# Host-laid inputs for the beginning, shift and scale in four parts, late roots in both norms

## The chip, the cores and the metric

The kernel runs on one core of one Trainium2 chip. The metric is the device time in microseconds (us) of one execution, as the median over runs; what is done to the inputs on the host before the launch is not in it. The engines of the core work side by side, each in its own queue's order: TensorE (matmul, transposes), VectorE, ScalarE, GpSimd (POOL) and SyncE (SP), which issues most of the loads.

## The reference, cut to what matters

One layer of a trunk over 512 latent tokens `x` and 256 context tokens `ctx`, 1024 channels. The condition vectors `c` and `c_ctx` give six modulation rows each (shift, scale, gate, twice). The parts that the change touches:

```python
mod  = split(silu(c) @ w_mod + b_mod, 6);  modc = split(silu(c_ctx) @ w_mod + b_mod, 6)
h    = modulate(rmsnorm(x, norm1_g), mod[0], mod[1])        # h * (1 + scale) + shift
hc   = modulate(rmsnorm(ctx, norm1_g), modc[0], modc[1])
u    = split(h @ w_in, ...)    ; uc = split(hc @ w_in, ...)   # mLSTM, attention, SSD, gates
y_m, y_a, y_s = mlstm(u, uc), diff_attention(u, uc), ssd(u, uc)
x    = x + mod[2] * (gated sum of y_m @ w_m, y_a @ w_a, y_s @ w_s) @ w_out
h2   = modulate(rmsnorm(x, norm2_g), mod[3], mod[4])
x    = x + mod[5] * conv_ffn(h2 @ w_up) @ w_down
rmsnorm(x, g) = x * rsqrt(mean(x * x) + 1e-6) * g
```

## The kernel before, in words

All large products keep f32 accuracy by splitting both factors into a high part in the short f32 format (fp32r) and a low rest, and adding three matmuls (high·high, high·rest, rest·high). A weight piece (`wpiece`, `wcol`, `wblk`) is loaded by SP into `wr` (two buffers), its high part `wh` is made by ScalarE (L171) and its rest `wl` by VectorE (L85); `wh` and `wl` have four buffers each. A helper records each operation, so nearly all matmuls have line L82, activations L104, two-input products L85, products with a scalar and a second input L88.

The beginning, lines 216 to 388, has these steps. The tokens come in rows (`xs`, three loads of 1 MB). Their squares are summed on ScalarE, the root is taken on VectorE (`rstd`, twelve small operations), the rows are scaled, and 48 transposes on TensorE turn them into columns (`xT`, channels on the partitions). Shift and scale need `silu(c) @ w_mod`: eight pieces of 0.5 MB (`wm`, five buffers) for each of two stages (NS = 2), multiplied with 32 columns of `scl` in 64 matmuls a stage, four of them side by side in strips of 32 rows. `h_part(n)` turns the sums into columns (`MT`, `A1`), and gives for each block of 128 channels k the high part of h (ScalarE) and the rest (VectorE), for the latent tokens (512 columns, `hlat`) and the context (256, `hctx`). Small parameters come by some twenty small loads (`crow`, `prm`, `wgr`) in rows, and are turned by three transposes (`PT`); the gate columns of `w_in` are copied one by one into a padded tile `wg`.

Four projections, called early, are begun while shift and scale are still being made: the gates (latent and context), a key column block (latent and context) and two query blocks (latent). Their matmuls for the k of stage n run beside the sums of stage n + 1 (`early(n)`). After them the mLSTM branch goes on with dense projections. The gate rows (`gate_rows`) run on VectorE and ScalarE beside these.

The second norm, lines 1118 to 1190: the output projection goes over blocks of 256 columns and token tiles j; each result is added to x1 on VectorE, and its squares are summed on ScalarE. `norm2(half)` takes the root for two token tiles, scales x1 into `xn`, transposes it (16 transposes a half) and makes high part and rest of h2 from the transposed tile. Half 0 is placed before the last block of the output projection, half 1 before the second half of the first four up projections, whose four banks (`fps`) are held until their convolutions have been read by VectorE. A tile `fc` for the last modulation row takes the buffer of `xn` (tag hc); its 16 products with w_mod run on VectorE beside the first up projections.

A list scheduler with a model of the engines places each operation in its engine's queue in the order in which it would be ready, with a higher priority for what stands in `tc.high_priority(...)`, and not before another one where `tc.issue_after(...)` says so. On the chip each queue is then worked off in that fixed order.

Of the kernel before, what the change touches and what calls it, by code (L numbers as in the profile page):

```python
# [18 lines left out]
P = 128  # L19
D = 1024  # L20
NK = D // P
T = 512
# [16 lines left out]
def build(tc, a, out):  # L39
# [150 lines left out]

    def proj_part(w, pl, pc, ks):
        hi, lo = w
        for k in ks:
            for n, (wt, v) in enumerate(((hi, 0), (hi, 1), (lo, 0))):
                st, sp_ = k == 0 and n == 0, k == NK - 1 and n == 2
                if pl is not None:
                    mm(pl, wt[:, k, :], hlat[v][:, k, :], st, sp_)
                if pc is not None:
                    mm(pc[:, 0:TC], wt[:, k, :], hctx[v][:, k, :], st, sp_)
# [12 lines left out]
    NS, NE, EX = 2, 3, 3  # L212
    W = D // NS
    KW, QW = W // P, W // 256

# [6 lines left out]

    last = [None, None]
# [3 lines left out]
    with pool("ph0", 1) as p0:  # L227

        crow = p0.tile([32, P], F32, name="crow")
        nc.sync.dma_start(crow[0:8, :], a["c"][0].rearrange("(r c) -> r c", c=P))  # L230
        nc.sync.dma_start(crow[8:16, :], a["c_ctx"].rearrange("(r c) -> r c", c=P))
        wv = w_in.rearrange("(k p) c -> p k c", p=P)
        wgr = wgp.tile([P, NK, 32], F32, name="wgr")
        nc.sync.dma_start(wgr[:, :, 0:16], wv[:, :, C_GM:C_GM + 16])
        nc.sync.dma_start(wgr[:, :, 16:32], wv[:, :, C_DT:C_DT + 16])
        xs = p0.tile([P, 6, D], F32, name="xs")
        for i in range(3):
            src = a["ctx"][0] if i == 0 else a["x"][0, (i - 1) * 256:i * 256]
            nc.sync.dma_start(xs[:, 2 * i:2 * i + 2, :], src.rearrange("(j p) c -> p j c", p=P))
            if i == 0:  # L240
                nc.sync.dma_start(crow[16:24, :], a["norm1_g"][0].rearrange("(r c) -> r c", c=P))
                nc.sync.dma_start(crow[24:32, :], a["norm2_g"][0].rearrange("(r c) -> r c", c=P))

        V.memset(scl, 0.0)
        tp = pss()
        PE.transpose(out=tp[:, 0:32], in_=crow, identity=ident[0:32, 0:32])
        act(scl[:, :, 0:2], tp[:, 0:16].rearrange("p (r k) -> p k r", r=2), AF.Silu)
        V.tensor_copy(NG, tp[:, 16:32])

        ssq = p0.tile([P, 6], F32, name="ssq")  # L250
        rs = p0.tile([P, 6], F32, name="rs")
        xT = p0.tile([P, NK, NT], F32, name="xT")
        for i in range(3):
            for t in (2 * i, 2 * i + 1):
                junk = p0.tile([P, D], mybir.dt.bfloat16, tag="junk", name="junk", bufs=1)
                act(junk, xs[:, t, :], AF.Square, accum=ssq[:, t:t + 1])
            rstd(rs[:, 2 * i:2 * i + 2], ssq[:, 2 * i:2 * i + 2], 2, 1.0 / D)
            for t in (2 * i, 2 * i + 1):
                ts(V, xs[:, t, :], xs[:, t, :], rs[:, t:t + 1])
            for k in range(0, NK, 2):  # L260
                tp = pss()
                for n in range(4):
                    PE.transpose(out=tp[:, n * P:(n + 1) * P], in_=xs[:, 2 * i + n % 2, (k + n // 2) * P:(k + n // 2 + 1) * P],  # L263
                                 identity=ident)
                o = xT[:, k:k + 2, i * 256:(i + 1) * 256]
                if k % 4:
                    V.tensor_copy(o, tp.rearrange("p (k c) -> p k c", k=2))
                else:
                    S.copy(o, tp.rearrange("p (k c) -> p k c", k=2))
# [4 lines left out]
        V.memset(wg, 0.0)  # L274
        prm = p0.tile([P, 3, P], F32, name="prm")
        V.memset(prm[:, 2, :], 0.0)
        V.memset(prm[96:128, 0, :], 0.0)

        def prow(which, r0, src):
            G.dma_start(prm[r0:r0 + src.shape[0], which, :], src)  # L280

        def rows(name):
            x = a[name][0]
            if len(x.shape) == 1:
                return x.rearrange("(r c) -> r c", c=P)
            return x.rearrange("k (r c) -> (k r) c", c=P)

        def grow(r, off, src):
            G.dma_start(prm[r:r + 1, 2, :].rearrange("o (d x) -> o d x", x=32)[:, off // 32:off // 32 + 2,
                                                                               off % 32:off % 32 + src.shape[2]], src)  # L290

        prow(0, R_BM, rows("b_mod"))
        prow(0, R_MCW, rows("m_conv_w"))
        prow(0, R_MCB, rows("m_conv_b"))
        prow(0, R_SCW, rows("s_conv_w"))
        prow(0, R_SCB, rows("s_conv_b"))

        prow(2, R3_G + 2, a["rowc"])
        grow(R3_G, 0, a["m_igate_b"])
        grow(R3_G, 64, a["m_fgate_b"])  # L300
        grow(R3_G, 72, a["s_dt_bias"])
        grow(R3_G + 1, 72, a["s_a_log"])
        fr = rows("ffn_conv_w")
        prow(2, 0, fr[128:132])
        prow(2, R3_MN, rows("m_norm_g"))
        prow(2, R3_SN, rows("s_norm_g"))
        prow(2, R3_SUB, a["a_subln_g"])
        prow(1, 0, fr[0:128])

        def pt(w):  # L310
            tp = pss()
            PE.transpose(out=tp[:, 0:P], in_=prm[:, w, :], identity=ident)
            V.tensor_copy(PT[:, w, :], tp[:, 0:P])

        for d in range(2):
            V.tensor_copy(wg[:, :, 32 * d:32 * d + 4], wgr[:, :, d * 8:d * 8 + 4])
            V.tensor_copy(wg[:, :, 64 + 32 * d:68 + 32 * d], wgr[:, :, d * 8 + 4:d * 8 + 8])
            V.tensor_copy(wg[:, :, 72 + 32 * d:80 + 32 * d], wgr[:, :, 16 + d * 8:24 + d * 8])
        split(wgh, wgl, wg)
        def h_part(n):  # L320

            ps = pss() if n else psl()
            for k in range(NK):
                r = p0.tile([P, 2, W], F32, tag="wm", name="wm", bufs=20 // QW // 2)
                last[0] = nc.sync.dma_start(r, a["w_mod"][0, k * P:(k + 1) * P, 0:2 * D]
                                            .rearrange("p (s c) -> p s c", s=2)[:, :, n * W:(n + 1) * W])
                for q in range(2 * QW):
                    last[1] = mm(ps[32 * q:32 * q + 32, 0:256], scl[:, k, :],
                                 r[:, q // QW, (q % QW) * 256:(q % QW + 1) * 256], k == 0, k == NK - 1)
                yield  # L330
            if n == 0:
                pt(0)
            R = 64 * QW
            m = p0.tile([P, 256], F32, tag="xw", name="msb", bufs=3)
            S.copy(m[0:R], ps[0:R, 0:256])
            tp = pss()
            for c in range(2):
                PE.transpose(out=tp[:, c * P:c * P + R], in_=m[0:R, c * P:(c + 1) * P], identity=ident[0:R, 0:R])
            ks = slice(n * KW, (n + 1) * KW)
            for s in (1, 0):  # L340
                for c in range(2):
                    tt(V, MT[:, s, ks].rearrange("p (q c) r -> p q c r", c=2)[:, :, c, :],
                       tp[:, c * P:c * P + R].rearrange("p (q r) -> p q r", r=32)[:, s * QW:(s + 1) * QW, 0:2],
                       PT[:, 0, s * 8 + n * KW:s * 8 + (n + 1) * KW].rearrange("p (q c) -> p q c", c=2)[:, :, c:c + 1]
                       .broadcast_to([P, QW, 2]), ALU.add)
            stt(A1[:, ks], MT[:, 1, ks], 1.0, NG[:, ks].unsqueeze(2).broadcast_to([P, KW, 2]), ALU.add, ALU.mult)
            for k in range(n * KW, (n + 1) * KW):
                for r, cs, h_ in ((0, slice(TC, NT), hlat), (1, slice(0, TC), hctx)):
                    hins[0] = act(h_[0][:, k, :], xT[:, k, cs], AF.Identity, scale=A1[:, k, r:r + 1], bias=MT[:, 0, k, r:r + 1])
                    ts(V, xT[:, k, cs], xT[:, k, cs], A1[:, k, r:r + 1], MT[:, 0, k, r:r + 1], ALU.mult, ALU.add)  # L350
                    tt(V, h_[1][:, k, :], xT[:, k, cs], h_[0][:, k, :].bitcast(F32), ALU.subtract)
            yield

        def early(n):

            for i, e in enumerate(first):
                if n == 0 and i:
                    for e_ in first[i + 1:i + 2]:
                        with tc.issue_after(last[0].ins):
                            e_[0] = wcol(e_[3])  # L360
# [921 lines left out]
```

## Time and profile before

| | |
|---|---|
| median of 3 runs | 1111.38 us (1109.24 to 1113.02) |
| profiled execution | 1112.19 us, span of its instructions 1110.4 us |
| TensorE / its weight loads | 1071.9 us (97%) / 939.2 us (85%) |
| VectorE / ScalarE / GpSimd | 714.6 us (64%) / 474.8 us (43%) / 78.7 us (7%) |
| mean granted TensorE clock | 0.993 |
| moved by DMA | 119.66 MB, 108 GB/s over the span |

An engine's share of busy time is a mean over stages that have different limits. The span is also shown in forty slices of 27.8 us; of these only the first shows TensorE far below nine tenths, four tenths. A row of the list in order of time has the start, the busy time, the engine, the line, the operation with what it writes and reads, the count, and in brackets how long the engine stood idle before it and what ended that.

### The profile page before, as it was taken

Reading aid. Unit: us, or ns where it says so; the run is one execution under the profiler, and the core shown is the slowest. Engines: PE = TensorE matmul, PEld = TensorE weight load, DVE = VectorE, ACT = ScalarE, POOL = GpSimd, SP = SyncE. Lnnn points to the kernel's source line nnn. Section 1 sums busy time; section 2 is a strip of 40 time slices with the busy share of each in tenths; the row PEclk is TensorE's granted clock in tenths of the full one; section 3 lists DMA queues with packets and bytes.
Section 4 is the critical chain, followed back from the end, with each engine's and each line's share of the span. In section 5 each row is a group of like instructions: output and inputs, shape, how many; then the busy total and the mean of one; then the engine's idle time right before and its main releaser. Section 6 shows DMA issues by size and latency. Waiting matters only on the chain.

```text
span 1110.4 us, 16645 instructions
## 1 busy us (share of the span) xinstructions
PE 1071.9 (97%) x6402; PEld 939.2 (85%) x6402; DVE 714.6 (64%) x1456; ACT 474.8 (43%) x887; POOL 78.7 (7%) x136
## 2 busy tenths in 40 slices
PE   4999999999999999999999899998999999999998
PEld 3598899988888999889998788997888888888887
DVE  6577676779757795856694558489766656642322
ACT  5465454557423333335744473344444343431110
POOL 3000000015231630000000000000000000000000
PEclk9899999999999999999999999999999999999999
DMA  8722222236545464321212104227333333323421
GB/s 296 245 77 77 82 58 60 74 90 184 162 151 160 143 182 115 90 82 39 60 52 80 57 20 143 86 77 231 111 95 95 95 94 96 97 93 97 133 94 38
DMA packets 140094, 119.66 MB, mean 108 GB/s; under 512 B 7025, under 2 KB 115928, under 8 KB 140016
## 3 DMA queue, kind: packets, MB, share of 16 engines
q1 hardware_dynamic: 139392, 118.28, 35.2%
q8 instruction: 50, 0.82, 0.3%
q0 software_dynamic: 624, 0.33, 0.3%
q14 instruction: 28, 0.23, 0.1%
HBM read 116.36 MB, written 2.23 MB: 107 GB/s over the span
## 4 chain that ended last, share of the span: by engine, by line
PE 87%; DVE 5%; ACT 3%; issue 2%; DMA 2%; SPq 0%; POOLq 0%; POOL 0%; DVEq 0%; ACTq 0%
PE pl L82 63%; PE psx L82 19%; PE sc L82 2%; ACT t L104 1%; DVE wl L85 1%; PE pl L946 1%; DVE t L88 1%; DMA wm<-in_w_mod_dram 1%; ACT wh L171 1%; PE psx L263 1%; DMA xs<-in_ctx_dram 0%; DVE rs L85 0%; ACT L104 0%; DVE t L94 0%; DMA xw<-in_a_lambda_dram 0%
## 5 line engine op out<-in xcount | busy, mean ns | idle before, releaser
L85 DVE TENSOR_TENSOR wl<-wr,wh 128x1024 fp32r<-128x1024 f32 x150 | 183.8, 1227 | 211.6 <-ACT wh L171 204.6
L171 ACT CAST wh<-wr 128x1024 fp32r<-128x1024 f32 x150 | 157.6, 1052 | 307.4 <-PE pl L82 214.1
L82 PE MATMUL pl<-h,wh 128*128 128x512 f32 (+1 forms) x768 | 222.3, 374 | 6.7 <-DVE ft L88 4.2
L82 PE MATMUL pl<-hl,wh 128*128 128x512 f32 x608 | 200.6, 399 | 0.4 <-ACT t L755 0.4
L82 PEld LDWEIGHTS pl<-h,wh 128*128 128x128 f32 x768 | 140.9, 189 | 32.6 <-issue 4.8
L82 PE MATMUL pl<-wh,hl 128*128 128x256 f32 x768 | 149.5, 288 | 0.0
L82 PE MATMUL pl<-h,wl 128*128 128x512 f32 (+1 forms) x384 | 143.2, 374 | 0.0
L82 PEld LDWEIGHTS pl<-hl,wh 128*128 128x128 f32 x608 | 112.9, 189 | 23.9 <-issue 1.6
L82 PEld LDWEIGHTS pl<-wh,hl 128*128 128x128 f32 x768 | 122.0, 191 | 0.7
L82 PE MATMUL pl<-hl,wl 128*128 128x512 f32 x304 | 120.7, 397 | 0.0
L82 PE MATMUL pl<-wl,hl 128*128 128x256 f32 x384 | 109.3, 285 | 0.0
L82 PEld LDWEIGHTS pl<-h,wl 128*128 128x128 f32 x384 | 72.7, 189 | 12.7
L82 PEld LDWEIGHTS pl<-wl,hl 128*128 128x128 f32 x384 | 73.4, 191 | 0.4
L82 PEld LDWEIGHTS pl<-hl,wl 128*128 128x128 f32 x304 | 57.4, 189 | 12.0
L82 PE MATMUL psx<-wh,ah 128*128 128x512 f32 (+1 forms) x176 | 66.5, 379 | 0.0
L82 PE MATMUL psx<-wl,ah 128*128 128x512 f32 (+1 forms) x176 | 66.2, 377 | 0.0
L82 PE MATMUL psx<-wh,al 128*128 128x512 f32 (+1 forms) x176 | 66.2, 376 | 0.0
L88 DVE SCALAR_TENSOR_TENSOR ft<-pl,PT,ft 128x511 f32<-128x511 f32 x88 | 65.3, 746 | 1.3
L82 PE MATMUL pl<-y,wh 128*128 128x512 f32 x192 | 60.0, 392 | 0.2 <-ACT y L104 0.2
L82 PE MATMUL psx<-wh,t 128*128 128x256 f32 x256 | 45.7, 281 | 0.0
L104 ACT ACTIVATE t<-t 128x512 f32<-128x512 f32 (+4 forms) x55 | 36.7, 682 | 19.3 <-DVE t L88 15.4
L82 PEld LDWEIGHTS pl<-y,wh 128*128 128x128 f32 x192 | 35.6, 188 | 7.5 <-ACT y L104 0.4
(301 smaller groups left out, 1844.9 us busy)
## 6 DMA issues: line engine op xcount, KB each, us to landing
wr<-in_w_in_dram SPq DMA_DIRECT2D x64, 512.0 KB, 4.2
wr<-in_w_up_dram SPq DMA_DIRECT2D x44, 512.0 KB, 3.7
t<-in_w_mod_dram SPq DMA_DIRECT2D x48, 256.0 KB, 4.5
wr<-in_w_down_dram SPq DMA_DIRECT2D x22, 512.0 KB, 3.6
wm<-in_w_mod_dram SPq DMA_DIRECT2D x16, 512.0 KB, 7.8
t<-nmd SPq DMA_DIRECT2D x24, 256.0 KB, 5.6
wr<-in_w_out_dram SPq DMA_DIRECT2D x8, 512.0 KB, 3.4
fc<-in_w_mod_dram SPq DMA_DIRECT2D x16, 256.0 KB, 3.2
```

The source lines that it names most:

```text
L82: return PE.matmul(o, l, r, start=start, stop=stop)
L85: eng.tensor_tensor(out=o, in0=x, in1=y, op=op)
L88: return V.scalar_tensor_tensor(out=o, in0=x, scalar=sc, in1=y, op0=op0, op1=op1)
L104: return S.activation(o, x, f, **kw)
L171: S.copy(hi, src)
L263: PE.transpose(out=tp[:, n * P:(n + 1) * P], in_=xs[:, 2 * i + n % 2, (k + n // 2) * P:(k + n // 2 + 1) * P], identity=ident)
L946: PE.transpose(out=tp[:, t * P:(t + 1) * P], in_=p0[:, (t0 + t) * P:(t0 + t + 1) * P], identity=ident)
```

## The change

The beginning reads four new arrays that the host lays out from the same inputs: `xt` (context and latent tokens, already transposed, 128 partitions x 8 x 768), `cols` (all small parameters as columns, with c, c_ctx and the norm gains in the last 32), `wm01` (shift and scale part of w_mod in four parts of two pieces of 1 MB, each contiguous per partition) and `wg` (the gate columns, padded). The transposes, the copies into `wg` and the small POOL loads of that stage are gone. Shift and scale are made in four stages (NS = 4), each for two blocks k. Squares and their sum over blocks are made on the transposed tokens; the sum over channels is six matmuls with `ones`. The root is applied late: a diagonal tile `dg` of the roots is multiplied with ones, which spreads each token's root over all partitions, and that is one factor of the product on VectorE. The second norm does the same: x1 is transposed without its root as each block is done, and the root comes in as a factor behind. The rest of h is made in one operation from x and shift. `load(e)` loads the weight piece of an early projection, and `ready(e, m, a)` makes its high part on ScalarE behind operation a and its rest on VectorE behind m. Cut to its core:

```diff
-    NS, NE, EX = 2, 3, 3
+    NS = 4
+    KW = NK // NS
...
+        nc.sync.dma_start(crow, a["cols"][:, 3 * P:3 * P + 32])
+        xT = p0.tile([P, NK, NT], F32, name="xT")
+        for k in range(0, NK, 2):
+            nc.sync.dma_start(xT[:, k:k + 2, :], a["xt"][:, k:k + 2, :])
+        nc.sync.dma_start(PT.rearrange("p w c -> p (w c)"), a["cols"][:, 0:3 * P])
...
+        for k in range(NK):
+            if k == 0:
+                act(acc, xT[:, k, :], AF.Square)
+            else:
+                q_ = p0.tile([P, NT], F32, tag="sq", name="sq", bufs=2)
+                act(q_, xT[:, k, :], AF.Square)
+                tt(V, acc, acc, q_, ALU.add)
+        sp = pss()
+        for t in range(6):
+            mm(sp[:, t:t + 1], acc[:, t * P:(t + 1) * P], ones)
+        rstd(rs, sp[:, 0:6], 6, 1.0 / D)
+        tt(V, dg, ident.unsqueeze(1).broadcast_to([P, 6, P]), rs.unsqueeze(2).broadcast_to([P, 6, P]), ALU.mult)
...
+        def load_m(n):
+            for h in range(2):
+                r = p0.tile([P, 4, 4 * P], F32, tag="wm", name="wm", bufs=6)
+                nc.sync.dma_start(r.rearrange("p k c -> p (k c)"), a["wm01"][n, h])
+                wms[n, h] = r
+        def sums(n, hold=None):
+            ps = psums[n] = pss()
+            with tc.issue_after(hold.ins) if hold is not None else ExitStack():
+                for k in range(NK):
+                    for q in range(4):
+                        lastm[0] = mm(ps[32 * q:32 * q + 32, 0:P], scl[:, k, :], wms[n, k // 4][:, k % 4, q * P:(q + 1) * P],
+                                      k == 0, k == NK - 1)
+        def h_part(n):
+            m = p0.tile([P, P], F32, tag="msb", name="msb", bufs=2)
+            S.copy(m, psums[n][:, 0:P])
+            tp = pss()
+            PE.transpose(out=tp[:, 0:P], in_=m, identity=ident)
...
+            for k in range(n * KW, (n + 1) * KW):
+                for r, cs, h_ in sides:
+                    rb = rsb[:, cs] if n else rsp[r][:, 0:cs.stop - cs.start]
+                    marks.append(stt(xT[:, k, cs], xT[:, k, cs], A1[:, k, r:r + 1], rb, ALU.mult, ALU.mult))
+                for r, cs, h_ in sides:
+                    hins.append(act(h_[0][:, k, :], xT[:, k, cs], AF.Identity, bias=MT[:, 0, k, r:r + 1]))
+                for r, cs, h_ in sides:
+                    marks.append(stt(h_[1][:, k, :], xT[:, k, cs], MT[:, 0, k, r:r + 1], h_[0][:, k, :].bitcast(F32),
+                                     ALU.add, ALU.subtract))
...
+        load_m(0)
+        nc.sync.dma_start(wg, a["wg"])
+        sums(0)
+        rsp = [pss(), pss()]
+        with tc.issue_after(lastm[0].ins):
+            mm(rsp[0], ones.broadcast_to([P, P]), dg[:, 2:6, :].rearrange("p t c -> p (t c)"))
+            mm(rsp[1][:, 0:TC], ones.broadcast_to([P, P]), dg[:, 0:2, :].rearrange("p t c -> p (t c)"))
+        split(wgh, wgl, wg)
+        load(first[1])
+        load(first[2])
+        load_m(1)
+        with tc.high_priority(1000):
+            h_part(0)
+        ready(first[1], marks[0], hins[1])
+        with tc.issue_after(hins[1].ins):
+            S.copy(rsb[:, TC:NT], rsp[0])
+            S.copy(rsb[:, 0:TC], rsp[1][:, 0:TC])
+        last = load(first[3])
+        ready(first[2], marks[-1], hins[3])
+        for n in range(NS):
+            if n + 2 < NS:
+                with tc.issue_after(last.ins):
+                    load_m(n + 2)
+            early(n, first[0:2 if n else 3])
+            if n == 0:
+                ready(first[3], marks[-1], hins[3])
+            if n + 1 < NS:
+                sums(n + 1, dense[0])
+                with tc.high_priority(1000):
+                    h_part(n + 1)
+                with tc.issue_after(lastm[0].ins):
+                    early(n, first[2 if n else 3:])
+            else:
+                early(n, first[2:])
...
-    xn = hp.tile([P, 4, D], F32, tag="hc", name="xn")
+    xt = hp.tile([P, NK, T], F32, tag="hc", name="xt")
+    def turn_x1(blk, js, tp):
+        for c in range(2):
+            for n, j in enumerate(js):
+                PE.transpose(out=tp[:, c * 256 + n * P:c * 256 + (n + 1) * P],
+                             in_=x1[j][blk // 2][:, (blk % 2) * 256 + c * P:(blk % 2) * 256 + (c + 1) * P], identity=ident)
+        S.copy(xt[:, 2 * blk:2 * blk + 2, js[0] * P:js[0] * P + 256], tp.rearrange("p (k c) -> p k c", k=2))
...
+        tt(V, dg, ident.unsqueeze(1).broadcast_to([P, 2, P]), rs2.unsqueeze(2).broadcast_to([P, 2, P]), ALU.mult)
+        rb = pss()[:, 0:256]
+        with tc.issue_after(behind.ins):
+            rbm = mm(rb, ones.broadcast_to([P, P]), dg.rearrange("p t c -> p (t c)"))
+        los = []
         for k in range(NK):
-            tp = pss() if half else psl()
-            for n, j in enumerate(js):
-                PE.transpose(out=tp[:, n * P:(n + 1) * P], in_=xn[:, j, k * P:(k + 1) * P], identity=ident)
-            t_ = nt()
-            act(h2h[:, k, hs], tp[:, 0:256], AF.Identity, scale=A2[:, k:k + 1], bias=MT[:, 2, k, 0:1])
-            ts(V, t_, tp[:, 0:256], A2[:, k:k + 1], MT[:, 2, k, 0:1], ALU.mult, ALU.add)
-            tt(V, h2l[:, k, hs], t_, h2h[:, k, hs].bitcast(F32), ALU.subtract)
+            t_ = xt[:, k, hs]
+            with tc.issue_after(los[-2].ins) if k > 1 else ExitStack():
+                stt(t_, t_, A2[:, k:k + 1], rb, ALU.mult, ALU.mult)
+            act(h2h[:, k, hs], t_, AF.Identity, bias=MT[:, 2, k, 0:1])
+            los.append(stt(h2l[:, k, hs], t_, MT[:, 2, k, 0:1], h2h[:, k, hs].bitcast(F32), ALU.add, ALU.subtract))
...
+            if j % 2:
+                with tc.high_priority(1000):
+                    turn_x1(blk, (j - 1, j), psl() if blk < 2 or js[0] == 0 else pss())
...
-    for half in range(2):
-        if half:
+    for n, (ps, w) in enumerate(zip(fps, fw)):
+        with tc.issue_after(rb1.ins) if n == 3 else ExitStack():
+            last_up = up_mm(ps, w, slice(0, 256))
+        if n == 1:
             with tc.high_priority(1000):
-                norm2(1, lambda: ft()[:, 0:256])
-        for ps, w in zip(fps, fw):
-            up_mm(ps, w, slice(half * 256, half * 256 + 256))
+                rb1 = norm2(1, last_up)
+    for ps, w in zip(fps, fw):
+        up_mm(ps, w, slice(256, 512))
```

## Rows read from the trace of the kernel before

**Rows 1.** The page's first part: busy us, share of the span, instructions, by engine.
```profile
PE 1071.9 (97%) x6402; PEld 939.2 (85%) x6402; DVE 714.6 (64%) x1456; ACT 474.8 (43%) x887; POOL 78.7 (7%) x136
```

**Rows 2.** Chain of waits, 0 to 100 us: start us, us, what.
```profile
2.60 5.52 DMA xs<-in_ctx_dram
...
15.03 3.67 PE psx L263 x16
...
23.36 7.03 DMA wm<-in_w_mod_dram
```

**Rows 3.** Windows, 0 to 40 us: us, engines' busy us, PEclk, DMA, GB/s.
```profile
12.00:15.00 3.00, 0.00 (x0) 0.00 (x0) 2.58 (x14) 2.94 (x5) 0.00 (x0) 1.00 1.05 407
...
20.00:21.00 1.00, 1.00 (x18) 0.48 (x11) 0.96 (x4) 0.00 (x0) 0.00 (x0) 1.00 0.09 31
...
30.00:31.00 1.00, 0.48 (x8) 0.23 (x8) 0.95 (x1) 1.00 (x3) 0.00 (x0) 0.67 1.05 408
...
36.00:37.00 1.00, 1.00 (x7) 0.83 (x4) 1.00 (x4) 0.00 (x0) 0.00 (x0) 0.50 1.06 398
```

**Rows 4.** Order of time, TensorE, 14.5 to 72 us: start us, us, instructions.
```profile
22.66 1.07 PE L82 MATMUL pl<-wm,scl 128*32 128x256 f32 x16
...
27.18 0.64 PE L82 MATMUL pl<-wm,scl 128*32 128x256 f32 x8
...
30.52 1.08 PE L82 MATMUL psx<-wm,scl 128*32 128x256 f32 x8 [1.77 <-DMA wm<-in_w_mod_dram]
31.53 0.80 PE L82 MATMUL pl<-hl,wgh 128*128 128x512 f32 x1
...
67.70 0.62 PE L82 MATMUL pl<-hl,wh 128*128 128x512 f32 x2
...
68.38 0.62 PE L82 MATMUL pl<-hl,wh 128*128 128x512 f32 x2
```

**Rows 5.** Groups by line and shape, 0 to 68 us: count, busy us, mean ns.
```profile
L85 DVE TENSOR_TENSOR wl<-wr,wh 128x1024 fp32r<-128x1024 f32 x6 | 7.3, 1224 | 5.7 <-ACT wh L171 5.7
...
L104 ACT ACTIVATE hl<-xT,MT,A 128x512 fp32r<-128x512 f32 x8 | 6.4, 805 | 1.2 <-DVE A L88 1.2
...
L104 ACT ACTIVATE junk<-xs 128x1024 bf16<-128x1024 f32 x6 | 6.3, 1055 | 1.5 <-DMA xs<-in_ctx_dram 1.3
...
L85 DVE TENSOR_TENSOR hl<-xT,hl 128x512 fp32r<-128x512 f32 x8 | 5.5, 684 | 0.0
...
L85 DVE TENSOR_TENSOR hct<-xT,hct 128x256 fp32r<-128x256 f32 x8 | 3.3, 418 | 0.0
```

**Rows 6.** Order of time, all engines, 0 to 80 us: the first root.
```profile
11.85 0.17 DVE L94 TENSOR_SCALAR rs<-ssq 128x2 f32<-128x2 f32 x1 [0.86 <-ACT junk L104]
...
14.22 1.42 DVE L92 TENSOR_SCALAR xs<-xs,rs 128x1024 f32<-128x1024 f32 x2
```

**Rows 7.** The tile ones: instructions that read it, ns min/median/max.
```profile
L82 PE MATMUL psx<-t,ones x4: 591/592/592, 280.5 to 305.1; 128*128 128x512 f32 x4
```

**Rows 8.** Order of time, TensorE, 96 to 125 us.
```profile
106.96 0.91 PE L82 MATMUL psx<-t,on 64*128 64x384 f32 x2 [1.74 <-DVE t L85]
```

**Rows 9.** Windows of 100 to 120 us.
```profile
110.00:112.00 2.00, 2.00 (x8) 1.71 (x8) 1.17 (x3) 0.88 (x2) 0.00 (x0) 0.50 0.72 234
```

**Rows 10.** Order of time, TensorE, 726 to 775 us.
```profile
734.69 0.50 PE L82 MATMUL pl<-h,wh 128*128 128x256 f32 x2 [2.49 <-DVE t L94]
...
759.18 0.40 PE L82 MATMUL pl<-h,wh 128*128 128x256 f32 x2
759.42 0.28 PE L82 MATMUL pl<-h,wl 128*128 128x256 f32 x1
763.87 0.91 PE L82 MATMUL pl<-h,wh 128*128 128x512 f32 x2 [4.17 <-DVE ft L88]
```

**Rows 11.** Order of time, VectorE, 717 to 775 us.
```profile
754.14 1.54 DVE L88 SCALAR_TENSOR_TENSOR fc<-fc,scl 128x512 f32<-128x512 f32 x2 [1.94 <-DMA fc<-in_b_mod_dram]
```

**Rows 12.** Windows of 756 to 770 us.
```profile
764.00:766.00 2.00, 2.00 (x6) 1.56 (x7) 2.00 (x4) 0.87 (x1) 0.00 (x0) 0.55 0.74 224
```

More of the change, by code (lines that the diff above doesn't have):

```diff
@@ L189, in wblk @@
         return [wpiece(w, 0, 4, c0, 256), wpiece(w, 4, 4, c0, 256)]
+    dense = [None]
     def proj_part(w, pl, pc, ks):
@@ L221, in build @@
     hctx = [hct[:, v] for v in range(2)]
-    last = [None, None]
+    NS = 4
+    KW = NK // NS
+    sides = ((0, slice(TC, NT), hlat), (1, slice(0, TC), hctx))
     wgs = ExitStack()
@@ L245, in build @@
[L245 to L250, printed above, removed]
-        rs = p0.tile([P, 6], F32, name="rs")
[L252 to L269, printed above, removed]
@@ new lines, in build, with banks, early, load @@
+        first = [[None, None, None, 0, True, True], [None, None, None, C_KM, True, True],
+                 [None, None, None, C_QM, False, False], [None, None, None, C_QM + P, False, False]]
+        def banks(e):
+            e[1] = (psl if e[4] else pss)()
+            e[2] = (psl if e[4] else pss)() if e[5] else None
+        def early(n, es_):
+            for e in es_:
+                proj_part(e[0], e[1], e[2], range(n * KW, (n + 1) * KW))
+        def load(e):
+            r = wp.tile([P, 1024], F32, tag="wr", name="wr", bufs=2).rearrange("p (k c) -> p k c", c=P)
+            e[0] = r
+            return nc.sync.dma_start(r, w_in.rearrange("(k p) c -> p k c", p=P)[:, :, e[3]:e[3] + P])
@@ L271, in build, with ready @@
+        def ready(e, m, m_act):
+            lo = wp.tile([P, 1024], F32R, tag="wl", name="wl", bufs=4).rearrange("p (k c) -> p k c", c=P)
+            hi = wp.tile([P, 1024], F32R, tag="wh", name="wh", bufs=4).rearrange("p (k c) -> p k c", c=P)
+            with tc.issue_after(m_act.ins):
+                S.copy(hi, e[0])
+            with tc.issue_after(m.ins):
+                tt(V, lo, e[0], hi.bitcast(F32), ALU.subtract)
+            e[0] = (hi, lo)
+        load_m(0)
         wg = wgp.tile([P, NK, P], F32, name="wg")
@@ L288, in grow @@
[L288 to L318, printed above, removed]
-        split(wgh, wgl, wg)
[L320 to L330, printed above, removed]
-            if n == 0:
[L332 to L360, printed above, removed]
-                if n == 0:
-                    e[1] = (psl if e[4] else pss)()
-                    e[2] = (psl if e[4] else pss)() if e[5] else None
-                for k in range(n * KW, (n + 1) * KW):
-                    with tc.issue_after(last[1].ins) if n < NS - 1 else ExitStack():
-                        proj_part(e[0], e[1], e[2], range(k, k + 1))
-                    yield
@@ L369, in build @@
-        first = [[(wgh, wgl), None, None, 0, True, True], [None, None, None, C_KM, True, True],
-                 [None, None, None, C_QM, False, False], [None, None, None, C_QM + P, False, False]][0:NE + 1]
-        hins = [None]
-        run(h_part(0))
-        with tc.issue_after(last[0].ins):
-            for e in first[1:2]:
-                e[0] = wcol(e[3])
-        for n in range(1, NS):
-            run(h_part(n), NK + EX, early(n - 1), KW * (NE + 1))
-        run(early(NS - 1))
-        with tc.issue_after(last[1].ins):
-            pt(1)
-            pt(2)
+        nc.sync.dma_start(wg, a["wg"])
@@ new lines, in build @@
+        ready(first[1], marks[0], hins[1])
[4 more added lines that the diff above has]
+        ready(first[2], marks[-1], hins[3])
+        for e in first:
+            banks(e)
+        for n in range(NS):
[3 more added lines that the diff above has]
+            early(n, first[0:2 if n else 3])
+            if n == 0:
+                ready(first[3], marks[-1], hins[3])
[7 more added lines that the diff above has]
+                early(n, first[2:])
@@ L1122, in norm2 @@
+    def norm2(half, behind):
+        js = slice(2 * half, 2 * half + 2)
         hs = slice(half * 256, half * 256 + 256)
-        rs2 = rsq2[:, 2 * half:2 * half + 2]
-        V.tensor_reduce(out=rs2, in_=ssq2[:, js[0]:js[0] + 2, :], op=ALU.add, axis=AX.X)
+        rs2 = rsq2[:, js]
+        V.tensor_reduce(out=rs2, in_=ssq2[:, js, :], op=ALU.add, axis=AX.X)
         rstd(rs2, rs2, 2, 1.0 / D)
-        for j in js:
-            for c in range(2):
-                ts(V, xn[:, j, c * 512:(c + 1) * 512], x1[j][c], rsq2[:, j:j + 1])
@@ L1272 @@
     feeds.update(_consts())
+    feeds.update(_layout(feeds))
+    for n in _LAID:
+        del feeds[n]
     arrays, aps = {}, {}
```

92 lines of the change are left out of this document (56 added, 36 removed).

## The prediction

> **What bounds the kernel now.** The busy shares come first: TensorE is busy for 97% of the span [rows 1]. A change can therefore only gain where TensorE waits, where its clock is low, or where it does work that goes away. The chain of waits shows the beginning as the largest such place: 5.5 us for the first megabyte of x, slow transposes, and 7.0 us for a load of w_mod [rows 2]. The windows tell why: the loads run at 407 GB/s, but in 20 to 21 us they fall to 31 GB/s, because the five wm buffers are full while the sums that empty them stand behind transposes in TensorE's queue; and from 30 to 37 us TensorE is granted 0.5 of its clock (1.2 GHz) after standing idle [rows 3]. The list in order of time gives the two ends of the stage: the first projection starts at 31.53 us, and the four early projections are done at 67.70 [rows 4]. Later waits are a 1.74 us one at 107 us, behind the gate rows [rows 8], and around the second norm 2.49 us at 734.7 and 4.17 us at 763.9 [rows 10], each followed or not by a low clock [rows 9, 12].
>
> Is the stage from 31.53 to 67.70 dense? Three 512-column matmuls take 0.68 us, 0.227 each [rows 4]; a 256-column one takes 0.12 (759.18 to 759.42 is two) [rows 10]. The four projections are 4 x 24 x 0.227 + 2 x 24 x 0.12 = 27.6 us. The second stage's sums, seven groups of eight at 0.067 a matmul [rows 4], add 3.8, transposes 0.6, and the half clock from 31.5 to 37 some 2.8: 34.8 of 36.2. So this stage hardly waits. What can be won is its start, less what four stages instead of two bring in waits.
>
> **The start.** Before the first projection the old kernel must have 3.15 MB of x, 4.19 MB of w_mod (half of shift and scale) and small pieces. The new one needs x and a quarter, 2.10 MB, plus 0.2 MB of parameters: 5.46 MB, two fewer. The first x load lands 5.52 us after its issue at 2.60; 1.05 MB at 407 GB/s are 2.6 of that, so 2.9 is start-up [rows 2, 3]. Now only one small load stands ahead, so x is issued at about 1.2. The four x loads (0.79 MB, 1.93 us each) land at 6.0, 8.0, 9.9, 11.8; the parameters at 12.3, the two halves of wm at 14.9 and 17.5.
>
> Two chains start from there. Norm: a Square of 768 columns is 0.8 us (1.055 for 1024), an add 0.95 (between 0.684 for 512 and 1.224 for 1024) [rows 5]; both keep pace with the loads, and the last add ends at 14.7. Six small sums at the slow pace of 0.23 (16 in 3.67) [rows 2]: 16.3 with handoffs. The root takes 2.35 (11.85 to 14.22) [rows 6]: 18.7. The diagonal product, one 768-wide op: 19.7. The f32 matmul that spreads it takes 0.59 at full clock [rows 7], about 1.0 at half: 20.7. Then the root product on VectorE 0.7, two activations 1.4 [rows 5]: 22.9.
> Shift and scale: data at 17.5, the last sixteen sums 1 to 2 us at half clock, 19.0. From the end of the first sums (27.82) to the first projection (31.53) the old kernel took 3.7 [rows 4], and the new one puts the root product between, 0.75: 23.5. The later chain decides: **first projection at 23.5** (bounds 22 to 25.5), 8.0 earlier.
>
> The Trainium skill (DMA: Bandwidth & Descriptors, section "Measured (HBM→SBUF, 128 partitions, SWDGE, issued from GpSimd)") gives 341 GB/s for a load of 1 MB and advises at least 1 MiB a load. By that figure, an estimate, 5.46 MB would take 2.6 us more than at 407 and the gain would be so much smaller. The trace does not agree: with loads of 0.5 and 1 MB queued it shows 407 GB/s [rows 3], so doubling the pieces is given neither a gain nor a loss.
>
> **From there to the end of the early projections.** Projections 27.6 as before. Three stages of sums, 32 matmuls of 128 columns each: if the cost goes by columns, half of 0.067, 1.1 us a stage; if by instructions, 2.2 [rows 4]. I take 1.8, 5.4 in all, since sums next to instructions this short are nearer to the upper row. Three transposes 0.4. **Clock**: the old kernel kept TensorE busy with transposes from 15 us, yet after 1.8 us without work it fell to 1.2 GHz for 6 us [rows 3, 4]. The new one does little before 23.5, so I take 4 us at half clock, 2.0 lost (0 to 3.3).
> **Waits**: in the first quarter VectorE has per k two root products and two subtractions, 2 x (0.684 + 0.418) = 2.2 us, 4.4 for its two k, and two weight splits of 1.224 [rows 5], 6.9 us, starting 1.6 before TensorE's 5.5 us of three projections: it ends about level, 1 us of waiting. Then sums of the next quarter, a copy, a transpose, two small ops, a product and an activation stand before the next k can be projected, about 3 us; in the first border only one projection's share, 6 x 0.227 = 1.4 us, covers them, later two, 2.7. Waits 1.6 + 0.3 + 0.3, with the fourth weight's late load (its buffer is the first one's) 0.3: together 3.5 (1 to 8).
> End at 23.5 + 27.6 + 5.4 + 0.4 + 2.0 + 3.5 = 62.4 against 67.7: **5.3 gained** (12 to a loss of 3). Of what is dropped, 48 x transposes, the copies, the gate pads and fifteen POOL loads, nothing counts again: they lay ahead of 31.5. All the later w_mod loads go on SP's queue behind the fourth weight; all 13.8 MB at 407 GB/s are in by 38 us, before their quarters need them.
>
> **The gate rows.** The 1.74 us wait at 107 us is VectorE's (gate rows and weight splits), and the clock is then 0.5 for 3 us [rows 8, 9], 1.7 lost. The gate projection now ends before two others (2.7 us and more ahead of the stage's end, with its own second k in front), about 1 us more lead. I take 1.0 of 3.4 (a loss of 1.5 to a gain of 3.4; the order on VectorE is planned anew).
>
> **The second norm.** x1 is transposed raw, per block, under the output projection; the 32 transposes are the same number. The root becomes a matmul of 256 columns, 0.39 us by the row for 512 [rows 7], twice: 0.8 lost on TensorE. VectorE loses the eight scalings of half a row each and gains two diagonal products of 0.4; per k two ops of 0.42 replace 0.5 and 0.38. So each half is ready about 1.5 us sooner, and the banks of the first up projection no longer wait for transposes to be read. Of the 2.49 us I take 1.5. Eight more copies on ScalarE, 0.6 each, lie beside TensorE's projections; without this cover a transpose that waits in TensorE's in-order queue for x1 stops it, 0.5.
> The 4.17 us wait is for a bank, released by convolution ops on VectorE, which stand among the fc sums of w_mod. These start at 754.14, since fc takes the place of xn, free only after the last transpose that reads it [rows 11]. In the new kernel the place is free after the second half's last subtraction, some 4 us sooner, so part of the fc sums is over when the convolutions come. The wait and the 0.55 clock behind it (1.7 more) [rows 12] cost 5.9; I take 2.5 back (a loss of 2 to a gain of 5.9). Sum: 1.5 + 2.5 - 0.8 - 0.5 = **2.7**.
>
> **Sum.** 5.3 + 1.0 + 2.7 = 9.0. The profiled execution took 1112.19 (span 1110.4, 1.8 around it): 1103.2. The three runs' median is 0.8 lower, so the forecast is **1102.5**, a likeliest range of 1097 to 1107.
>
> **Rivals.**
> A, the start wins in full: TensorE is at 2.4 GHz when the projections begin and the borders are covered (waits 1, clock 0, sums 3.4), end at 56; with the 763.9 wait gone, 11.7 + 1 + 5 = 17.7: 1094. For it: a 2.49 us wait at 734.7 was followed by no low clock [rows 10]. Against: [rows 3]. Chance 0.18.
> B, the first quarter goes by VectorE, ScalarE and the half clock (waits 8, clock 3.3, sums 6.6), and the second norm only evens out: 23.5 + 27.6 + 6.6 + 0.4 + 3.3 + 8 = 69.4, but a start at 22 gives 67.9, no gain, with 1 to 3 elsewhere: 1109. For it: VectorE is as loaded as TensorE there. Against: only one quarter is. Chance 0.15.
> C, slower: at each of the three quarter borders TensorE stands idle about 1.8 us, as before 30.5, and the clock falls each time. A border then costs 1.8 + 2.8 = 4.6, three 13.8, and with sums by instructions (6.6) the end is 23.5 + 27.6 + 6.6 + 0.4 + 2 + 13.8 = 73.9, 6.2 late; with 2 back in the second norm and 0.8 for the median 1115.6. It decides from about 3.7 us lost per border. For it: [rows 3, 4] show just this once. Against: other projections can be put in between. Chance 0.10.
> The Trainium skill (TensorE: Matmul & The Clock Gate, section "What's actually happening") says that the throttled state is the default and activity releases it; by that rule every border that leaves TensorE idle is a risk of C's kind. The trace bears this out at 30 us and not at 734.7.
>
> The likeliest case has 0.57. About 0.3%, 3.3 us, is what a measurement here can tell from no change. Faster by more: the likeliest and A nearly whole, a third of B: 0.80; within: 0.11; slower: 0.09. The range that holds 8 in 10 is 1094 to 1110.5.
>
> **What would show it.** Right: first projection at 22 to 25.5 us, the load rate unbroken near 400 GB/s up to 25 us, the first 512-column projections past the early four at 59 to 65 us, waits before the up projections under 1.5 and 2.5 us. Wrong: a clock of 0.5 after each quarter's sums, projections starting after 27 us, or a wait longer than 4.2 us where the convolutions release the banks.

## The result, and the profile after

The changed kernel is slower, and the forecast was wrong in sign.

| | us, median | runs | lowest to highest | profiled execution (span) |
|---|---|---|---|---|
| before | 1110.31 | 4 | 1109.04 to 1113.02 | 1112.19 (1110.4) |
| changed | 1116.91 | 4 | 1116.40 to 1118.51 | 1116.58 (1114.8) |
| forecast | 1102.5 | | 1094 to 1110.5 | |

The ratio is 1.0052, 95% interval 1.0033 to 1.007. A later group of runs gave 1116.88 beside 1111.83 (1.0048, 1.0031 to 1.0065).

The list in order of time of TensorE, 22 to 74 us (start us, us, instruction, idle before it), answers to [rows 4]:

```profile
24.66 0.50 PE L82 MATMUL pl<-hl,wgh 128*128 128x512 f32 x1 [1.99 <-ACT hl L104]
...
32.97 1.95 PE L82 MATMUL psx<-wm,scl 128*32 128x128 f32 x64
...
42.69 1.96 PE L82 MATMUL psx<-wm,scl 128*32 128x128 f32 x64
...
47.47 0.27 PE L277 MATMUL psx<-ident,msb 128*128 128x128 f32 x1
...
49.73 0.50 PE L82 MATMUL pl<-hl,wgh 128*128 128x512 f32 x1 [2.00 <-ACT hl L104]
...
56.26 1.95 PE L82 MATMUL psx<-wm,scl 128*32 128x128 f32 x64
...
61.01 0.27 PE L277 MATMUL psx<-ident,msb 128*128 128x128 f32 x1
...
63.27 0.50 PE L82 MATMUL pl<-hl,wgh 128*128 128x512 f32 x1 [1.99 <-ACT hl L104]
...
72.06 0.66 PE L82 MATMUL pl<-hl,wh 128*128 128x512 f32 x2
```

The first projection starts at 24.66, 6.9 us earlier than before. The four early projections end at 72.06, 4.4 later than the 67.70 of [rows 4]. So 11 us go away in between. At the second and the third quarter border TensorE's transpose (L277) comes late, and 2.26 us pass from each to the next projection, 2.0 of them idle. ScalarE had copied the sums long before, as its own list shows:

```profile
45.48 0.26 ACT L275 COPY msb<-psx 128x128 f32<-128x128 f32 x1
...
58.34 0.27 ACT L275 COPY msb<-psx 128x128 f32<-128x128 f32 x1 [7.20 <-PE psx L82]
```

The copies are done at 45.74 and 58.61, the transposes that read them start at 47.47 and 61.01. What stands between in TensorE's in-order queue is the whole share of the last two early projections, the very work that was to cover the transpose and what follows it. Windows of the stage and of three stretches in it (us, busy us of TensorE, its weight loads, VectorE, ScalarE, POOL, granted clock, DMA share, GB/s) show the second part of the loss:

```profile
24.66:71.99 47.33, 41.00 (x339) 32.67 (x340) 22.77 (x45) 16.40 (x29) 0.85 (x3) 0.89 0.41 144
...
28.00:30.00 2.00, 2.00 (x8) 1.71 (x7) 1.77 (x3) 0.65 (x1) 0.00 (x0) 0.50 0.35 77
52.00:54.00 2.00, 2.00 (x6) 1.54 (x6) 0.50 (x2) 0.00 (x0) 0.00 (x0) 0.50 0.00 0
66.00:68.00 2.00, 2.00 (x6) 1.53 (x5) 0.41 (x4) 0.20 (x1) 0.85 (x3) 0.50 0.00 0
```

TensorE is idle for 47.33 - 41.00 = 6.3 us of the stage, and it loses 11% of 47.33, 5.2 us, to the lower clock (1.2 GHz), which in this execution sets in 1 to 2.5 us after the end of each of the 2.0 us waits.

Around the second norm the wait of 2.49 us [rows 10] is gone, a new one of 1.55 has come, and the convolution's wait has gone from 4.17 to 3.60. TensorE, 733 to 769 us, then VectorE, 731 to 764:

```profile
733.85 0.70 PE L82 MATMUL psx<-xw,ones 128*128 128x256 f32 x2 [1.55 <-DVE xw L85]
...
767.99 1.19 PE L82 MATMUL pl<-h,wh 128*128 128x512 f32 x2 [3.60 <-DVE ft L88]
```

```profile
731.90 1.23 DVE L85 TENSOR_TENSOR wl<-wr,wh 128x1024 fp32r<-128x1024 f32 x1 [0.89 <-ACT wh L171]
...
733.38 0.41 DVE L85 TENSOR_TENSOR xw<-ident,rsq 128x256 f32<-128x256 f32 x1
...
756.50 0.48 DVE L88 SCALAR_TENSOR_TENSOR h<-xt,MT,h 128x256 fp32r<-128x256 f32 x1 [0.18 <-ACT h L104]
761.40 1.54 DVE L88 SCALAR_TENSOR_TENSOR fc<-fc,scl 128x512 f32<-128x512 f32 x2 [4.42 <-DMA fc<-in_b_mod_dram]
762.86 1.22 DVE L85 TENSOR_TENSOR wl<-wr,wh 128x1024 fp32r<-128x1024 f32 x1
763.99 0.74 DVE L88 SCALAR_TENSOR_TENSOR ft<-pl,PT,ft 128x511 f32<-128x511 f32 x1
```

The root's matmul waits because its diagonal product (733.38) stands behind a weight split. The fc sums start at 761.40, not before 754.14 [rows 11]: fc takes the place of the transposed x1, which VectorE now reads to the norm's end (756.98), so its load lands 4.42 us after that, and the convolution (ft) is queued behind.

### The profile page after: what moved, and what is told of

The parts are those of the page before. It is cut to its first block, busy times and chain, and to the rows that moved or that the text cites. A ratio compares the mean times of both kernels' runs of the same rounds, so it can differ in the third digit from the quotient of the medians.

```text
span 1114.8 us, 16735 instructions
## 1 busy us (share of the span) xinstructions
PE 1071.5 (96%) x6498; PEld 944.0 (85%) x6498; DVE 709.4 (64%) x1408; ACT 473.7 (42%) x888; POOL 71.7 (6%) x121
## 4 chain that ended last, share of the span: by engine, by line
PE 86%; DVE 8%; ACT 3%; issue 1%; DMA 1%; SPq 0%; DVEq 0%; ACTq 0%
PE pl L82 61%; PE psx L82 20%; PE sc L82 2%; DVE t L88 2%; DVE wl L85 1%; PE pl L924 1%; ACT t L104 1%; DVE t L521 1%; DVE t L85 1%; DVE xT L88 1%; DMA xT<-in_xt_dram 1%; DVE acc L85 1%; ACT wh L171 0%; ACT L104 0%; PE pl L891 0%
## 5 line engine op out<-in xcount | busy, mean ns | idle before, releaser
L171 ACT CAST wh<-wr 128x1024 fp32r<-128x1024 f32 x147 | 154.2, 1052 | 295.8 <-PE pl L82 220.3
```

Source lines behind the costliest of these rows:

```text
L171: S.copy(hi, src)
```

## The experiments

"Before" is the kernel before on the same chip in the same group: 1112.8 for the first eight, 1111.8 for the last four. A ratio is to it, with its 95% interval; 0.001 is 1.1 us.

**e1 and e2: which half loses.** The two parts of the change, one at a time.

```diff
 # e1: as changed, but for the second norm
-    xt = hp.tile([P, NK, T], F32, tag="hc", name="xt")
+    xn = hp.tile([P, 4, D], F32, tag="hc", name="xn")
...
 # e2: as before, but for the second norm
-    xn = hp.tile([P, 4, D], F32, tag="hc", name="xn")
+    xt = hp.tile([P, NK, T], F32, tag="hc", name="xt")
...
```

> The changed beginning with the second norm of before. Theory (the loss is made at the quarter borders of the beginning: 6.3 us without work and 5.2 us of half clock between the first projection at 24.7 us and the end of the early projections at 72.0): all of the loss is here, some 4.5 to 6.5 us more than before, 1115 to 1117.5. Rival (the late root in the second norm costs half of it or more): 1113 or less.

Measured: 1118.99, ratio 1.0058 (1.0037 to 1.0079). The new beginning alone loses as much as the whole change. Not all of that is lost in the beginning itself: in this trace the early projections end 3.7 us late (71.42 against 67.70), and some 3 us more come at the second norm of before, where TensorE waits 5.13 us for the convolution (4.17 in [rows 10]).

> The beginning of before with the changed second norm. Theory: the second norm by itself is worth 0 to 1 us, 1109 to 1111 (the forecast's term was 2.7 us, which would give 1107.6). Rival (it costs): 1113 or more.

Measured: 1109.67, ratio 0.9967 (0.9954 to 0.9979): 3.7 us gained, a miss for the expectation and more than the 2.7 of the forecast. Its trace has waits of 1.56 and 2.32 us where [rows 10] have 2.49 and 4.17, and a clock of 1.00 from 725 to 775 us where the kernel before has 0.97, 1.5 us in 50. With the new beginning the same norm is worth 0.7 to 1.1 us (1.0058 against 1.0052 and 1.0048), which the intervals don't tell from nothing.

**e3: the transpose first.** Three of the covering matmuls, then the transpose, then the rest.

```diff
-            PE.transpose(out=tp[:, 0:P], in_=m, identity=ident)
+            turned[0] = PE.transpose(out=tp[:, 0:P], in_=m, identity=ident)
...
-                with tc.issue_after(lastm[0].ins):
-                    early(n, first[2 if n else 3:])
+                parts = [(e, k) for e in first[2 if n else 3:] for k in range(n * KW, (n + 1) * KW)]
+                for i, (e, k) in enumerate(parts):
+                    with tc.issue_after(turned[0].ins if i else lastm[0].ins):
+                        proj_part(e[0], e[1], e[2], range(k, k + 1))
```

> As changed, but at each quarter border only the first three of the last early matmuls stand ahead of the transpose of the sums in TensorE's queue, the others behind it. Theory: the two waits of 2.0 us at 49.7 and 63.3 us fall to under 0.8, the clock no longer falls behind them (1.7 us each), 6 to 7 us less, 1109 to 1111.5. Rival (four stages cost by their number, or the first quarter does): the waits move, 1115 to 1117.

Measured: 1112.98, ratio 0.9999 (0.9987 to 1.0011). By the ratios the order alone is worth 0.005, 5.5 us, and takes the loss back. Waits of TensorE, 22 to 72 us (us in total, times, longest), and a window from the first border to the end of the stage, in which the changed kernel falls to 0.50 twice:

```profile
PE pl L82 <- ACT hl L104: 3.1, 3, 2.0
PE pl L82 <- DVE hl L88: 0.8, 2, 0.4
PE psx L279 <- ACT msb L277: 0.7, 2, 0.4
```

```profile
31.00:72.00 41.00, 38.35 (x347) 30.51 (x346) 22.39 (x43) 16.30 (x27) 0.85 (x3) 1.00 0.49 166
```

The waits for ScalarE's hl were four and 6.6 us; the one of 2.0 that is left is the start's, and the clock still falls behind it (0.50 in 28 to 30 us).

**e4: fill the waits.** Nothing is moved; eight matmuls whose result nobody reads stand behind the transposes of quarters 0, 2 and 3.

```diff
+            if n in (0, 2, 3):
+                with tc.issue_after(turned[0].ins):
+                    for _ in range(8):
+                        mm(psums[n], wgh[:, 0, :], wgh[:, 0:4, :].rearrange("p k c -> p (k c)"))
```

> As changed, with eight more matmuls of 512 columns (1.8 us, their result is not used) behind the transpose at the start and at the second and third border, where TensorE stood idle 2.0 us. Nothing on the path gets shorter, only the idle time is filled. Theory that the granted clock is a cost of its own: it stays at 2.4 GHz there, 1.7 us at each of three places, 3.5 to 5 us less, 1112 to 1113.5. Rival (only the idle time costs, the clock does not fall for it): 1116.5 to 1118.

Measured: 1114.27, ratio 1.0013 (1.0002 to 1.0024): about 4 us come back. The data come no sooner (2.26 us from the last transpose to its projection, as before), but the granted clock is 1.00 from 20 to 76 us, 0.91 in the changed kernel. So the clock's fall is a price of its own, near the 5.2 us read above.

**e5: the fc sums behind the convolutions.**

```diff
+        gated = V.tensor_tensor(out=cv[0], in0=cv[0], in1=cv[1], op=ALU.mult)
+        hold5 = gated if f == 1 else hold5 if f else None
...
-            next(md, None)
+            with tc.issue_after(hold5.ins):
+                next(md, None)
```

> The changed kernel, with VectorE's multiply-adds for the last modulation vector (fc<-fc,scl) held behind the first two gated convolutions. Theory: the second norm's missing gain sits here. In the changed kernel VectorE ends the norm at 756.98, then stands 4.42 us in front of the first fc sum, whose load can only begin once the norm's tile is read to the end, and the convolution that frees TensorE's banks is queued behind it; TensorE waits 3.60 us and then runs about 4 us at the lower clock (some 1.7 us lost). With the sums behind, the convolution begins near 757 and the first bank is free by 760, before TensorE runs dry at 764.4: 4 to 5 us come back, 1112 to 1113 beside 1116.9. Rival 1: the convolution waits for its own banks, which are full only when the second halves are multiplied: 0 to 1 us. Rival 2: the sums, moved later, hold w_down at the end: nothing gained or slower.

Measured: 1110.29, ratio 0.9988 (0.9973 to 1.0003): 6 to 7 us by the medians, more than expected. Part of that is not the edit's. The profiled execution has the same beginning as the second run of the changed kernel (e9 below: last transpose of the sums at 59.11 and 59.15 us) and is 4.9 us shorter (spans 1107.3 and 1112.2), which is the 4 to 5 expected. The convolution's wait falls to 0.98 us and no lower clock follows. What VectorE waits for now is the next weight split:

```profile
758.28 1.23 DVE L85 TENSOR_TENSOR wl<-wr,wh 128x1024 fp32r<-128x1024 f32 x1 [4.57 <-ACT wh L171]
759.42 0.74 DVE L88 SCALAR_TENSOR_TENSOR ft<-pl,PT,ft 128x511 f32<-128x511 f32 x1
```

**e6: the splits behind the diagonal product.**

```diff
-        tt(V, dg, ident.unsqueeze(1).broadcast_to([P, 2, P]), rs2.unsqueeze(2).broadcast_to([P, 2, P]), ALU.mult)
+        dgi[0] = tt(V, dg, ident.unsqueeze(1).broadcast_to([P, 2, P]), rs2.unsqueeze(2).broadcast_to([P, 2, P]), ALU.mult)
...
-        fw.append(w_up(*x))
+        with tc.issue_after(dgi[0].ins):
+            fw.append(w_up(*x))
```

> The changed kernel, with the weight splits of the first four w_up pieces held behind the diagonal product of the first root on VectorE. Theory: the root's matmul waits 1.55 us because its diagonal product stands behind a 1.23 us weight split; without the split in front the wait falls to about 0.3 and the time by 1.0 to 1.5 us (some 1115.5 beside 1116.9). Rival: the splits, now later, are what the first w_up matmuls wait for, and the time is unchanged or up to 1 us longer.

Measured: 1114.12, ratio 1.0018 (1.0001 to 1.0034). The wait goes from 1.55 to 0.74, 0.8 us; the medians differ by some 3, which this wait does not explain and which stays open. Executions of the same beginning differ by as much (by place, below).

**e7: e3 with filling matmuls in the first quarter only** (e4's lines with `n == 0`).

> The changed kernel with the transpose of each quarter's sums ahead of the covering matmuls (as in the run with the transpose alone, 1112.98) and 8 matmuls without use behind the first quarter's transpose, so that TensorE does not stand idle 2.0 us ahead of the first early projection. Theory: the lower clock after that idle time costs 1.4 to 1.7 us (granted clock 0.62 to 0.66 and 0.50 in 26:30), the gate rows that set the first decay sums start that much earlier and the time falls by as much, to some 1111.3. Rival: the chain of the gate rows on VectorE sets the later time and takes the gain: unchanged, 1113.0.

Measured: 1112.18, ratio 0.9995 (0.9982 to 1.0008): at most a small gain over e3, as the rival had it. The clock no longer falls at 26 us, but the matmul behind the gate rows starts at 107.65 (107.38 in e3) after 2.52 us of waiting for VectorE. The gain is gone before that: at the second border the transpose now waits 1.62 us (0.36 in e3), since the copy of the sums stands on ScalarE behind a weight cast that waits for its load, and the early projections end at 67.28 (67.00 in e3). So the rival's number came true, and not by the gate rows alone.

**e8 and e12: all four edits; e12 also holds the next weight splits behind the first convolution.**

```diff
 # e12, beside e8
-                up_mm(ps, w_up(f, ct), slice(0, T))
+                with tc.issue_after(cv0[0].ins), tc.issue_after(cv0[1].ins), tc.high_priority(1000 if f == 2 else 0):
+                    w_ = w_up(f, ct)
+                up_mm(ps, w_, slice(0, T))
```

> The changed kernel with all four edits: transpose first, 8 filling matmuls in the first quarter, the fc sums behind the first two convolutions, the weight splits behind the first diagonal product. If the four add: 1116.9 less 5.9, 1.5, 4.5 and 1.2, some 1104, near what was forecast for the change itself (1102.5), and under the kernel before by 0.7%. Rival: the edits meet the same later waits and the time is 1108 to 1111.

Measured: 1108.98, ratio 0.9967 (0.9952 to 0.9981). Under the kernel before, but the four do not add: 1104 was the sum.

> All four edits of the run before (1108.98), and the splits of the next w_up pieces behind the first convolution, on ScalarE and VectorE. In that run VectorE waits 4.57 us for a weight split that ScalarE can only begin when TensorE has done with the old piece (754.90), and the first convolution is queued behind it; TensorE waits 0.99 us. With the convolution first the bank is free some 2 us earlier: 0.7 to 1.0 us come back, 1108. Rival: the split, now later, is what TensorE waits for: 1109 or 1110.

Measured: 1107.88, ratio 0.9968 (0.9955 to 0.9981), the same as e8 by the ratio. TensorE has no wait at the convolution any more.

**e9: the changed kernel again.**

> The changed kernel once more, unedited, so that the edited ones of this group stand beside it on one chip: 1116.9 to 1118 beside 1112.8 for the kernel before, a ratio of 1.004 to 1.006. Every theory expects the same here.

Measured: 1116.88, ratio 1.0048 (1.0031 to 1.0065).

**e10 and e11: without the new beginning.** e10 is e2 with the edits of e5 and e6; e11 is the kernel before with e5's edit alone.

> The beginning of the kernel before, with the new second norm and its two edits (fc sums behind the first two convolutions, weight splits behind the first diagonal product). Theory: the new norm with the old beginning gave 1109.67; the sums' wait and the clock after it give 2 to 4 us more here, the split about 1: 1105 to 1107. Beside the run with all four edits (1108.98) this prices the new beginning once its order is mended: if it is worth its earlier start (some 2 us at the first decay sums), the old beginning should be slower than that run; if the old beginning is as fast or faster, the new one gains nothing even in a good order.

Measured: 1106.09, ratio 0.9951 (0.9937 to 0.9965), the fastest of all.

> The kernel before with one edit: the fc sums behind the first two convolutions. Theory: the wait of the convolution (4.17 us there, and the lower clock after it) stood in the kernel before for the same reason, a load that waits for the norm's tile and VectorE's queue behind it, so 2.5 to 5 us come back without any of the change: 1108 to 1110 beside 1112.8. Rival: there the norm's tile was read out 6 us earlier and the sums are not what the convolution waits for: 0 to 1 us.

Measured: 1106.33, ratio 0.9954 (0.994 to 0.9968). The theory's upper end: 5.5 us by the medians (3.6 to 6.7) from one order on VectorE in the kernel before. The waits of TensorE from 715 to 1085 us are now:

```profile
PE pl L82 <- DVE t L94: 2.5, 1, 2.5
PE pl L82 <- DVE ft L88: 0.4, 1, 0.4
```

So the 4.17 us wait and the clock behind it were worth about what the prediction priced them at (5.9; by place, below, 3.9 in the one trace), but they were not the norm's to remove: with the sums out of the way, the new norm and its split edit (e10) add 0.2 us by the medians, which is nothing within the intervals, though its own 2.5 us wait is down to 0.7. And against e10 the mended new beginning (e8, e12) is some 1.8 us slower, if anything (the intervals overlap a little), and not faster.

**By place.** One matmul stands in every trace, some 27 us behind the gate rows' (`psx<-t,t`, 128x130; in the kernel before it starts at 134.25). How late it starts tells what the beginning and the gate rows lost, and the rest of the difference of the spans what came behind (us, against the kernel before, one profiled execution each):

| | changed | e9 | e1 | e3 | e4 | e5 | e6 | e7 | e8 | e12 | e2 | e10 | e11 |
|---|---|---|---|---|---|---|---|---|---|---|---|---|---|
| late there | 4.1 | 2.1 | 3.5 | 0.9 | 2.0 | 2.0 | 5.9 | 1.1 | -0.1 | 0.1 | 0.9 | -1.1 | -0.8 |
| rest of the span | 0.3 | -0.3 | 3.2 | -0.4 | -1.9 | -5.1 | -0.9 | -1.0 | -5.2 | -4.4 | -3.4 | -5.2 | -3.9 |

The changed kernel loses its time ahead of this matmul, and its second norm gives nothing. The same beginning is 2.0 to 5.9 us late in five executions (changed, e9, e1, e5, e6), the old one -1.1 to 0.9 (e2, e10, e11): one profile places a loss, but does not size it to better than 1 or 2 us. The mended beginnings (e8, e12) are level with the old ones and not ahead of them.

## Why the prediction was wrong

**The step that failed** is the one under "Waits": "in the first border only one projection's share, 6 x 0.227 = 1.4 us, covers them, later two, 2.7. Waits 1.6 + 0.3 + 0.3". The chain (copy, transpose, two small ops, product, activation) takes 0.4 us from the sums' end to the copy's at the third border (1.1 at the second, where a weight cast stands before the copy on ScalarE) and 2.26 from the transpose on, 2.7 to 3.4 where I gave 3. So its size was right, and the cover was there, but I set it beside the chain without asking where in TensorE's queue the transpose stands. It stood behind the cover. Border 1, the one I thought worst, cost 1.4 us and no clock; borders 2 and 3, priced at 0.3 each, cost 2.0 of waiting and some 1.7 of clock each. e3 changes nothing but this place and takes the loss back.

Term by term, for the end at 62.4 forecast and 72.0 measured:

- First projection 23.5 forecast, 24.66 measured (1.2), inside the bounds. The two chains and the load order came as described; this step holds. The lateness begins with the root's six sums: they leave twelve records and took 2.72 us, where six at 0.23 were counted, and the first sums of shift and scale stand behind them in TensorE's queue, from 17.46 on.
- Sums of three stages 5.4, measured 1.95 + 1.96 + 1.95 = 5.9 (0.5). Near by luck: the 0.067 of [rows 4] is the price of a record of 256 columns, and a stage's 32 matmuls leave 64 records, two each (in the kernel before as well, where a stage has 32 matmuls and not 64). At 30 ns a record of 128 columns the price went by columns, the case that I had at 1.1 a stage.
- Clock 2.0, measured 5.2 (3.2): three falls, where I had one. In e9 there are two falls, and 3.4 us are lost.
- Waits 3.5, measured 6.3 (2.8).
- The rest, 1.9: most of it was in front of me, since I had found 34.8 of the old stage's 36.2 us and left the missing 1.4 out of the new sum.

**Gate rows**, 1.0 forecast. The wait fell from 1.74 [rows 8] to 1.05 and the lower clock of [rows 9] did not come (1.00 from 107 to 160 us, 0.97 before), but a wait of 1.37 us at 138 (0.39 before) took most of it: the matmul behind it is 4.1 us late, the stage's end was 4.4. The mended beginnings show why an early end is worth little: in e3 the early projections end 5.0 us sooner than in the changed kernel and the matmul behind the gate rows only 3.3, waiting 2.51 us for VectorE; in e8 2.54.

**Second norm**, 2.7 forecast. Its first wait gave 0.9 instead of 1.5, since VectorE's weight split took the place of the banks. For the 4.17 us wait I expected that "the place is free after the second half's last subtraction, some 4 us sooner"; the sums start 7.3 us later, 3.3 once the 4.0 by which all is late there are taken off (761.40 against 754.14). In the kernel before the place was free after the last transpose, ahead of the last subtractions; now it is read by those as well. Alone the norm gained 3.7 (e2), for a reason that was not mine: a shorter wait without the clock's fall after it. Why the same code kept less of it behind the new beginning I can't settle. The fc load landed 3.13 us after the norm in e2 and 3.94 to 4.42 in the two runs of the changed kernel, but 3.17 and 3.28 in e7 and e4, which have the same norm behind the new beginning: it differs between executions, and the beginning alone does not set it.

**The rivals.** C was the case, with a chance of 0.10: 1115.6 against 1116.9. Its mechanism is right at two of three borders, at 3.7 us each where it said 4.6, just the point from which it decides; the first border, better covered by order, is the exception. That its number came so near is partly luck: it has 13.8 for the borders, where 1.4 + 3.7 + 3.7 = 8.8 were measured, and 2 back in the second norm, where nothing came. The rule of the Trainium skill that stood beside it (TensorE: Matmul & The Clock Gate, section "What's actually happening"), that the throttled state is the default and activity releases it, agrees with the clock of 0.50 after borders 2 and 3 and with e4, where work without use keeps it at 1.00; e9's start, a wait as long with no fall behind it, shows that a wait need not bring the fall. A fails at the borders, B at the first quarter, where TensorE waits only 0.5 us for ScalarE's weight copy.

## What to carry over

Work covers a chain only if every link of the chain that runs on the covering engine stands ahead of that work in the engine's queue; price a border by the order of the queue, not by the sum of what is available. Before crediting a change with a wait near it, ask what is queued in front of the instruction that ends the wait: here it was a row of sums waiting for a load, and moving them behind the convolutions gained 3.6 to 6.7 us with no other change. An earlier stage is worth only what the next in-order chain (here VectorE's gate rows) lets through.

## What had not been expected of the hardware

The lower clock does not follow a wait every time, nor always at the same distance. In the second run of the changed kernel (e9) the first projection waits 1.99 us as in the first run, and so on at the borders (6.8 us in total against 6.6). Three windows of it, behind the start and the second and third border, and then one of e1 behind its second border, where TensorE had waited 2.00 us up to 50.48:

```profile
27.00:30.00 3.00, 3.00 (x20) 2.66 (x19) 2.86 (x4) 1.75 (x4) 0.00 (x0) 1.00 0.28 71
48.50:51.50 3.00, 3.00 (x8) 2.52 (x9) 2.71 (x6) 1.35 (x3) 0.00 (x0) 0.50 0.43 143
62.00:65.00 3.00, 3.00 (x10) 2.42 (x9) 2.55 (x8) 2.30 (x4) 0.21 (x1) 0.50 0.00 0
```

```profile
51.00:54.00 3.00, 2.60 (x15) 2.12 (x15) 2.24 (x5) 0.89 (x2) 0.00 (x0) 1.00 0.01 2
```

At e9's start there is no fall, where the first run has 0.50, and none behind e1's second border. The two falls of e9 cost as much as those of the first run, some 1.7 us each, but one comes sooner: the matmul that ends the wait at the second border, at 48.45, is already slow (0.79 us), where the first run's, at 49.73, is not (0.50). The early projections of e9 ended 2.0 us sooner (69.81 against 71.82 for the same matmul), and the missing fall is most of that. The times of one kernel lie up to 8 us apart (1107.4 to 1115.9 in 35 runs of the kernel before), so a single profile can be off by as much as a term of the sum.
